# The router's columns as the stationary operand for six of eight token blocks

## The chip, the core and the metric

One NeuronCore of a Trainium2 chip runs the whole program. TensorE (PE; its weight loads are listed apart as PEld) multiplies, VectorE (DVE), ScalarE (ACT) and GpSimd (POOL) work on tiles in SBUF and PSUM, and SyncE (SP) issues most DMAs. The metric is the device time of one execution in microseconds (us), lower is better.

## The reference, cut to what matters

One encoder layer over 1024 tokens of width 1024, all in float32: differential attention, then a hierarchical mixture of 16 experts in four groups, then a final norm. The change touches the router, which turns each token's normed and modulated row into 4 group logits and 16 expert logits:

```python
def hier_moe(h, w_rg, b_rg, w_re, b_re, w_gate, w_up, w_down):
    t = h.reshape(B * S, D)
    g_logits = (t @ w_rg).astype(jnp.float32) + b_rg
    g_idx = jnp.argmax(g_logits, axis=-1)
    e_logits = jnp.einsum('td,dge->tge', t, w_re).astype(jnp.float32) + b_re
    e_sel = jnp.take_along_axis(e_logits, g_idx[:, None, None], axis=1)[:, 0]
    top_v, top_i = lax.top_k(e_sel, EXPERT_TOP_K)
```

The logits of a token pick one group and two of its experts, so nothing of the experts can begin before the last token's logits have been ranked and the tokens have been gathered.

## The kernel before, in words

Tokens are worked in 8 blocks of 128 (`t` = 0 to 7, `TB` = 8). Attention runs first (up to about 650 us). The stage in question, the generator `post_gen` (from L657), follows and runs to about 740 us; its first pieces are interleaved with the last of attention. For each block t it does:

- `chunk(t, 0)` and `chunk(t, 1)`: the output projection of one half of 512 columns. Each is 24 matmuls on 128x512 (L693) into one of two PSUM buffers `mm`; then DVE does L702, L703, L704 (gate, residual, scale) and ACT squares the rows for the norm (L705, L707 or L709 and L710). The row's reciprocal root `r` comes out of the second half alone.
- `trans(t - 1, 0)` and `trans(t - 1, 1)`, between the two halves of block t: PE turns over the eight 128x128 pieces of the block before (L722), the first four into the PSUM buffer `tp`, the other four into the PSUM buffer `av`; ACT copies each four to `h2T` in SBUF (L723, `Q<-tp` and `Q<-av`). `tp` and `av` are one buffer each.
- `router(t - 1)`, after the second half: eight matmuls in full float32, each two passes in the records (16 records, L735). `h2T[:, k]`, 128 tokens, is the stationary operand and the 20 router columns `wr20[:, k]` move; the result, 128 tokens x 20, goes to `tp`. DVE scales it by `r`, adds the bias and writes `L[:, t]` (L737).
- `write_h2(t - 1)`: DVE finishes the normed rows (L729) and SP stores them (L730).

Block 7 is cut finer: after `chunk(7, 0)` and the turn-over of block 6 the second half goes in two quarters (`last_sums`, L806, 24 matmuls of 256 columns each), and `routing()` is stepped in between. Its `ranks(0, 6)` (L922 to L928) ranks the logits of blocks 0 to 5 on DVE; matmuls L954 to L959 on PE count them and need L928's result; then come the turn-over of half of block 7 (L826), the router of block 6 (L735 into `av`), and the second quarter. Blocks 6 and 7 are ranked at the end, then the tokens of expert 0 are gathered.

What sets the order: PE runs in the order in which the code is written, with no exception (`manual_schedule` on PE for the whole program). DVE, ACT, POOL and SP are ordered by a list scheduler with a cost model, except in the last stretch (from L795), where ACT and DVE too keep the order of the code. Every engine takes its instructions in order, so that an instruction that waits holds up those behind it.

Of the kernel before, what the change touches and what calls it, by code (L numbers as in the profile page):

```python
# [4 lines left out]
F32 = mybir.dt.float32  # L5
# [5 lines left out]
OP = mybir.AluOpType  # L11
# [4 lines left out]
P = 128  # L16
S = 1024
D = 1024
KT = D // P
TB = S // P  # L20
# [15 lines left out]
def build(tc, x, c, ada_w, ada_b, norm_mix, norm_ffn, w_in, lq1, lk1, lq2, lk2, subln, w_out,  # L36
          rgw, rgb, rew, reb, wg, wu, wd, norm_final, out, dbg=None):
    nc = tc.nc
# [21 lines left out]
    ident = const.tile([P, P], F32, name="ident")  # L60
# [19 lines left out]
    st = tc.alloc_tile_pool(name="start", bufs=1)  # L80
# [4 lines left out]
    def ps_mm():  # L85
        return ps.tile([P, 512], F32, name="mm", bufs=2)

    def ps_tp():
        return ps.tile([P, 4, P], F32, name="tp")

    def ps_av():
        return ps.tile([P, 512], F32, name="av")
# [108 lines left out]
    for t in range(TB):  # L201
# [8 lines left out]
        for kk in range(2):  # L210
# [4 lines left out]
            for i in range(4):  # L215
                k = kk * 4 + i
# [124 lines left out]
    at = tc.alloc_tile_pool(name="attn", bufs=1, reuse_waits="tile")  # L341
# [97 lines left out]
    now = [0]  # L439
# [217 lines left out]
    def post_gen():  # L657
        st = {}
# [20 lines left out]
            nc.scalar.copy(oH, orw)  # L679
            (nc.vector if t in OLD else nc.gpsimd).tensor_tensor(oL, orw, f(oH), op=OP.subtract)  # L680

        L = RT0["L"] = at.tile([P, TB, 20], F32, name="L", tag="vt")
        cst = at.tile([P, 3, D], F32, name="K", bufs=2)
        load(0, 0)
        load(1, 0)
# [10 lines left out]
        def chunk(t, n, py=None):  # L696
            ns = slice(n * 512, (n + 1) * 512)
            if py is None:
                py = ps_mm()
                yield from sums(t, n, py, range(H))  # L700
            a, xt, sq, rst = st[t][2:6]
            nc.vector.tensor_tensor(a[:, ns], py, g1b[:, ns], op=OP.mult)  # L702
            nc.vector.tensor_tensor(xt[:, ns], xt[:, ns], a[:, ns], op=OP.add)  # L703
            nc.vector.tensor_tensor(a[:, ns], xt[:, ns], s2b[:, ns], op=OP.mult)  # L704
            nc.scalar.activation(py, xt[:, ns], AF.Square, accum_out=sq[:, n:n + 1])  # L705
            if n == 0:
                nc.scalar.activation(sq[:, 0:1], sq[:, 0:1], AF.Identity, scale=1.0 / D, bias=epst)  # L707
            else:
                nc.scalar.activation(rst, sq[:, 1:2], AF.Ln, scale=1.0 / D, bias=sq[:, 0:1])  # L709
                nc.scalar.activation(rst, rst, AF.Exp, scale=-0.5)  # L710
                nc.sync.dma_start(accd[t * P:(t + 1) * P], xt)
# [15 lines left out]
        def write_h2(t):  # L727
            a, rst = st[t][2], st[t][5]
            nc.vector.scalar_tensor_tensor(a, a, rst, sh2b, op0=OP.mult, op1=OP.add)  # L729
            nc.sync.dma_start(h2d[t * P:(t + 1) * P], a)  # L730

        def router(t, ks, pl):
            h2T = st[t][6]
            for k in ks:
                nc.tensor.matmul(pl, h2T[:, k], wr20[:, k], start=(k == 0), stop=(k == KT - 1))  # L735
            if k == KT - 1:
                nc.vector.scalar_tensor_tensor(L[:, t], pl, st[t][5], br20, op0=OP.mult, op1=OP.add)  # L737
            for k in ks:
                yield

        def pl_tp():
            return ps_tp().rearrange("p a b -> p (a b)")[:, 0:20]

        def load_next(t):

# [18 lines left out]
        def block(t):  # L764
            if t == 0:
                yield from first()
                return
            yield from chunk(t, 0)
            yield from trans(t - 1, 0)
            yield from trans(t - 1, 1)  # L770
            if t < TB - 1:
                yield from chunk(t, 1)
                yield from router(t - 1, range(KT), pl_tp())
                write_h2(t - 1)

        for t in range(TB):
# [9 lines left out]
            for _ in block(t):  # L786
                if t:
                    load_next(t + 1)
                yield
        t = TB - 1  # L790
        a, xt, sq, rst = st[t][2:6]
        rt = routing()
        next(rt)
# [27 lines left out]
        h2T = at.tile([P, KT, P], F32, name="Q", bufs=3)  # L821
# [15 lines left out]
        pl = ps_mm()[:, 0:20]  # L837
# [14 lines left out]
    RT0 = {}  # L852
# [154 lines left out]
    wr20 = misc.tile([P, KT, 20], F32, name="wr20")  # L1007
    nc.sync.dma_start(wr20[:, :, 0:4], rgw[0].rearrange("(k p) g -> p k g", p=P))
    nc.sync.dma_start(wr20[:, :, 4:20], rew[0].rearrange("(k p) g e -> p k (g e)", p=P))
    br20 = misc.tile([P, 20], F32, name="br20")  # L1010
# [12 lines left out]
    n = 5  # L1023
# [7 lines left out]
    for i, (h, qb) in enumerate(seq):  # L1031
# [6 lines left out]
        n = RATE.get(i, n)  # L1038
# [685 lines left out]
```

## Time and profile before

| what | value |
|---|---|
| device time, median of 3 runs | 1216.61 us (1216.36 to 1218.6) |
| the profiled execution | 1216.69 us, of which the recorded span is 1214.9 us |
| PE busy | 1107.9 us, 91% of the span |
| PE weight loads busy | 917.9 us, 76% |
| DVE busy | 942.5 us, 78% |
| ACT busy | 727.2 us, 60% |
| POOL busy | 262.4 us, 22% |
| mean granted clock of PE | 0.962 |

The times in the rows are us from the span's start. The share of a whole span hides that stages have different limits: the stage of the change is the stretch from 650 to 741 us and is read by itself. Matmul records are pipelined, so that a record is longer than its share of the engine; the spacing between the starts of weight loads (PEld) says what one costs. [...]

### The profile page before, as it was taken

What the parts mean: (1) busy time and instruction counts of PE and PEld (TensorE: products, weight loads), DVE (VectorE), ACT (ScalarE), POOL (GpSimd) and SP (SyncE); (2) the same over time, 40 slices, a digit from 0 to 9 for tenths busy, and PEclk for the clock granted to TensorE, in tenths of its full rate; (3) what the DMA queues carried; (4) which work ended last, traced back from release to release, by engine and by line L of the source; (5) the groups of instructions that cost most, each with busy time, mean ns of one, the idle gap of its engine ahead of it and who ended that gap; (6) DMA issues with size and microseconds to landing.
All of it is one profiled execution on the core that took longest, in us unless ns stands there. A gap on an engine that the chain in (4) does not pass through costs nothing. (4 is left out here: it accounts for less than half of the span.)

```text
span 1214.9 us, 19164 instructions
## 1 busy us (share of the span) xinstructions
PE 1107.9 (91%) x6760; PEld 917.9 (76%) x6760; DVE 942.5 (78%) x1560; ACT 727.2 (60%) x1206; POOL 262.4 (22%) x283
## 2 busy tenths in 40 slices
PE   4889999999999999999889995999999999999990
PEld 3667877777787787777678885887888887888880
DVE  5969789888888777687884657798877898777774
ACT  5566666757666676767664323566565667455563
POOL 3011011111101111113402402433222232222121
PEclk8899999999999999999899996899999999999995
DMA  9712022322323110112407734699979899877745
GB/s 328 216 53 82 23 87 87 90 86 83 99 92 89 46 40 27 29 42 91 143 27 226 264 121 147 220 333 336 294 225 303 252 345 336 280 228 227 217 132 223
DMA packets 153255, 199.55 MB, mean 164 GB/s; under 512 B 12967, under 2 KB 124232, under 8 KB 153138
## 3 DMA queue, kind: packets, MB, share of 16 engines
q1 hardware_dynamic: 146432, 179.86, 45.3%
q0 software_dynamic: 6512, 17.68, 6.1%
q8 instruction: 63, 1.03, 0.3%
q10 hardware_dynamic: 194, 0.54, 0.1%
q14 instruction: 54, 0.44, 0.1%
HBM read 175.77 MB, written 27.67 MB: 167 GB/s over the span
## 5 line engine op out<-in xcount | busy, mean ns | idle before, releaser
L1122 DVE TENSOR_TENSOR wlo<-wraw,whi 128x1024 fp32r<-128x1024 f32 x187 | 224.7, 1231 | 23.9 <-ACT whi L1117 13.9
L1385 PE MATMUL gu<-whi,XT 128*128 128x256 f32 x1216 | 209.6, 285 | 2.7
L1117 ACT CAST whi<-wraw 128x1024 fp32r<-128x1024 f32 x192 | 193.2, 1049 | 7.7 <-ACTq L1540 5.0
L486 ACT ACTIVATE E<-E,mn 128x1024 f32<-128x1024 f32 x128 | 147.1, 1151 | 83.3 <-DVE mn L483 83.1
L1385 PEld LDWEIGHTS gu<-whi,XT 128*128 128x128 f32 x1216 | 172.5, 191 | 9.9 <-issue 6.2
L483 DVE CUSTOM_DVE_ANT_0 E<-S,negd 128x1024 f32<-128x1024 f32 x128 | 152.8, 1219 | 18.9 <-PE S L478 18.2
L1385 PE MATMUL gu<-wlo,XT 128*128 128x256 f32 x704 | 148.4, 289 | 1.9 <-POOL wlo L1122 1.9
L285 PE MATMUL mm<-hH,wh 128*128 128x512 f32 x336 | 139.3, 415 | 2.1 <-DVE V L384 2.1
L285 PE MATMUL mm<-hL,wh 128*128 128x512 f32 x336 | 140.3, 417 | 0.0
L285 PE MATMUL mm<-hH,wl 128*128 128x512 f32 x336 | 138.8, 413 | 0.0
L143 POOL TENSOR_TENSOR wl<-wraw,wh 128x1024 fp32r<-128x1024 f32 x21 | 50.4, 2401 | 325.8 <-ACT wh L142 285.5
L513 ACT CAST aH<-tp 128x512 fp32r<-128x512 f32 x128 | 74.0, 578 | 73.9 <-PE tp L511 73.7
L1385 PEld LDWEIGHTS gu<-wlo,XT 128*128 128x128 f32 x704 | 109.8, 191 | 2.4 <-POOL wlo L1122 2.1
L497 DVE SCALAR_TENSOR_TENSOR E<-E,r 128x1024 f32<-128x1024 f32 x64 | 85.8, 1340 | 27.8 <-ACT E L495 26.3
L514 DVE TENSOR_TENSOR aL<-tp,aH 128x512 fp32r<-128x512 f32 x128 | 87.9, 687 | 17.3 <-ACT aH L513 16.1
L1417 PE MATMUL py<-whi,hid 128*128 128x512 f32 x256 | 92.1, 422 | 4.1 <-ACT hid L1407 1.4
L511 PE MATMUL tp<-ident,E 128*128 128x128 f32 x512 | 78.9, 277 | 10.4 <-DVE aL L514 7.2
L511 PEld LDWEIGHTS tp<-ident,E 128*128 128x128 f32 x512 | 62.5, 142 | 33.5 <-DVE aL L514 13.6
L693 PE MATMUL mm<-wo,wh 128*128 128x512 f32 x240 | 80.1, 408 | 1.3 <-ACT mm L705 1.3
L285 PEld LDWEIGHTS mm<-hH,wh 128*128 128x128 f32 x336 | 63.5, 189 | 18.3 <-issue 5.1
L285 PEld LDWEIGHTS mm<-hH,wl 128*128 128x128 f32 x336 | 63.5, 189 | 17.1 <-issue 7.9
L285 PEld LDWEIGHTS mm<-hL,wh 128*128 128x128 f32 x336 | 63.4, 189 | 16.9 <-issue 8.0
(342 smaller groups left out, 2230.2 us busy)
## 6 DMA issues: line engine op xcount, KB each, us to landing
wraw<-in_expert_w_gate SPq DMA_DIRECT2D x64, 512.0 KB
wraw<-in_expert_w_up SPq DMA_DIRECT2D x64, 512.0 KB
wraw<-in_expert_w_down SPq DMA_DIRECT2D x64, 512.0 KB
aw<-in_ada_w SPq DMA_DIRECT2D x64, 256.0 KB
wraw<-in_attn_w_in SPq DMA_DIRECT2D x23, 512.0 KB
ld<-in_ada_w SPq DMA_DIRECT2D x32, 256.0 KB
ld<-in_x SPq DMA_DIRECT2D x8, 512.0 KB
xt<-in_x SPq DMA_DIRECT2D x8, 512.0 KB
```

Of the source, the lines that this page charges most:

```text
L285: nc.tensor.matmul(pq, w[:, k], t[k][:, n], start=(k == 0 and i == 0), stop=(k == KT - 1 and i == 2))
L483: nc.vector.tensor_tensor_reduce(out=e, in0=sps[m], in1=negd[:, w0:w0 + S], op0=OP.add, op1=OP.min, scale=-slope, scalar=3.0e38, accum_out=mn)
L486: nc.scalar.activation(e, e, AF.Exp, bias=mn, scale=-1.0, accum_out=sm)
L497: nc.vector.scalar_tensor_tensor(es[0], es[1], r2, es[0], op0=OP.mult, op1=OP.add)
L511: nc.tensor.transpose(pt[:, i], a[:, k * P:(k + 1) * P], ident)
L513: nc.scalar.copy(th[:, kk * 4:kk * 4 + 4, q], pt)
L514: nc.vector.tensor_tensor(tl[:, kk * 4:kk * 4 + 4, q], pt, f(th[:, kk * 4:kk * 4 + 4, q]), op=OP.subtract)
L693: nc.tensor.matmul(py, w[:, h], wt[h][:, ns], start=(h == 0 and s == 0), stop=(h == H - 1 and s == 2))
L1117: nc.scalar.copy(WP[e, i][0], RAW[e, i])
L1122: eng.tensor_tensor(low, RAW[e, i], f(high), op=OP.subtract)
L1385: nc.tensor.matmul(pg[:, i], XT[:, xi, k], w[:, k % 4], start=(k == 0 and xi == 0 and wi == 0 and i == 0), stop=(k == KT - 1 and (xi, wi) ...
L1417: nc.tensor.matmul(py[n], hT[:, xi, i], WP[e, 8 + hf * 2 + i][wi][:, n * 512:(n + 1) * 512], start=(hf == 0 and j == 0), stop=(hf == 1 and ...
```

## The change

For blocks 0 to 5 the roles in the router's matmul are exchanged. `router_t` holds the 20 columns of `wr20[:, k]` in the array and moves the 128 tokens of `h2T[:, k]` past them, so that the result is 20 x 128 in `tp`; ACT copies it to a strip of SBUF (`lts`, two places in turn). One block later `logits` turns the strip over on PE (a transposition of 20 x 128 to 128 x 20), and DVE reads that as L737 did before. The transposition stands between `trans(t - 1, 1)` and `chunk(t, 1)` and goes to `av`; that of block 5 stands after the turn-over of block 6, ahead of `routing()`. Blocks 6 and 7 keep the old form. The strip and `L` share one tile.

```diff
-        L = RT0["L"] = at.tile([P, TB, 20], F32, name="L", tag="vt")
+        lts = at.tile([P, 512], F32, name="L", tag="vt")
+        L = RT0["L"] = lts[:, 0:TB * 20].rearrange("p (t n) -> p t n", t=TB)
...
+        def router_t(t):
+
+            h2T = st[t][6]
+            pl = ps_tp().rearrange("p a b -> p (a b)")
+            for k in range(KT):
+                nc.tensor.matmul(pl[0:20, 0:P], wr20[:, k], h2T[:, k], start=(k == 0), stop=(k == KT - 1))
+                yield
+            lt = lts[0:20, 256 + t % 2 * P:256 + t % 2 * P + P]
+            nc.scalar.copy(lt, pl[0:20, 0:P])
+            LT[t] = lt
+
+        def logits(t):
+            pl = ps_av()[:, 0:20] if now[0] >= 65 else ps_tp().rearrange("p a b -> p (a b)")[:, 0:20]
+            nc.tensor.transpose(pl, LT[t], ident[0:20, 0:20])
+            nc.vector.scalar_tensor_tensor(L[:, t], pl, st[t][5], br20, op0=OP.mult, op1=OP.add)
+
+        LT = {}
+
...
-        def pl_tp():
-            return ps_tp().rearrange("p a b -> p (a b)")[:, 0:20]
...
             if t < TB - 1:
+                if t - 2 in LT:
+                    logits(t - 2)
                 yield from chunk(t, 1)
-                yield from router(t - 1, range(KT), pl_tp())
+                yield from router_t(t - 1)
                 write_h2(t - 1)
...
         t = TB - 1
+        logits(t - 2)
         a, xt, sq, rst = st[t][2:6]
         rt = routing()
         next(rt)
```

In the changed program the lines behind the edit have other numbers: L722 is L723, L693 is L694, the transposition is L746, the DVE step behind it L747, the ACT copy of the strip L741, and `ranks` is L941 to L947.

PE, between the two halves of block 2, before (the waits are those on other engines' semaphores; `av<-ident,hrow` is the second half of the turn-over):

```order
L693 MATMUL mm<-wo,wl 128x512
L722 MATMUL tp<-ident,hrow 128x128 [waits DVE_49]
L722 MATMUL tp<-ident,hrow 128x128 x3
L722 MATMUL av<-ident,hrow 128x128 [waits DVE_49]
L722 MATMUL av<-ident,hrow 128x128 x3
L693 MATMUL mm<-wo,wh 128x512 [waits Activation_49]
L693 MATMUL mm<-wo,wh 128x512
```

The same place on PE in the changed program:

```order
L694 MATMUL mm<-wo,wl 128x512
L723 MATMUL tp<-ident,hrow 128x128 [waits Activation_49]
L723 MATMUL tp<-ident,hrow 128x128 x3
L723 MATMUL av<-ident,hrow 128x128 [waits DVE_49]
L723 MATMUL av<-ident,hrow 128x128 x3
L746 MATMUL av<-ident,L 128x20 [waits Activation_49]
L694 MATMUL mm<-wo,wh 128x512 x2
```

One instruction has come in, it writes the buffer that the four ahead of it wrote, and it waits for ACT. It stands at this place six times (in blocks 2 to 6 and ahead of L806 in block 7).

DVE, in blocks 6 and 7, before: from the logits of block 5 (L737) to the first steps on `chunk(7, 0)`, with `ranks(0, 6)` (L922 to L928) between them:

```order
L737 SCALAR_TENSOR_TENSOR L<-tp,r_6786,br_738 128x20
L703 TENSOR_TENSOR xt<-xt,hrow 128x512
L922 TENSOR_TENSOR K<-L 128x480
L704 TENSOR_TENSOR hrow<-xt,K 128x512
L923 TENSOR_TENSOR K<-L 128x480
L924 TENSOR_TENSOR K<-K 128x480
L925 TENSOR_TENSOR K<-K 128x480
L926 TENSOR_REDUCE K<-K 128x120
L927 TENSOR_TENSOR K<-K 128x120
L928 TENSOR_TENSOR rk<-K 128x96
L702 TENSOR_TENSOR hrow<-mm,K 128x512
L703 TENSOR_TENSOR xt<-xt,hrow 128x512
```

DVE in the changed program, from the last step on `chunk(7, 0)` (L705) over the logits of block 5 (L747) to the end of `ranks(0, 6)`; L826 to L828 are the steps of the first quarter:

```order
L705 TENSOR_TENSOR hrow<-xt,K 128x512
L747 SCALAR_TENSOR_TENSOR L<-av,r_6795,br_738 128x20
L941 TENSOR_TENSOR K<-L 128x480
L942 TENSOR_TENSOR K<-L 128x480
L943 TENSOR_TENSOR K<-K 128x480
L826 TENSOR_TENSOR hrow<-mm,K 128x256
L944 TENSOR_TENSOR K<-K 128x480
L827 TENSOR_TENSOR xt<-xt,hrow 128x256
L945 TENSOR_REDUCE K<-K 128x120
L828 TENSOR_TENSOR hrow<-xt,K 128x256
L946 TENSOR_TENSOR K<-K 128x120
L947 TENSOR_TENSOR rk<-K 128x96
```

The ranks of six blocks stood ahead of DVE's steps on `chunk(7, 0)`; now they stand behind them, mixed with those of the first quarter. On PE the matmuls that need them (L954 before, L973 now) still stand right behind the first quarter.

## Rows read from the trace of the kernel before

**Rows 1.** By stretch: us, busy PE, PEld, DVE, ACT, POOL (instructions), clock, DMA, GB/s.

```profile
650.00:700.00 50.00, 50.00 (x277) 43.12 (x277) 27.54 (x29) 19.13 (x41) 17.49 (x7) 1.00 0.84 273
700.00:739.00 39.00, 39.00 (x249) 34.46 (x247) 22.31 (x40) 10.88 (x28) 2.39 (x1) 1.00 0.27 99
...
741.00:775.00 34.00, 19.85 (x136) 18.20 (x136) 28.56 (x72) 13.41 (x22) 18.86 (x27) 0.60 0.56 180
775.00:1198.00 423.00, 388.22 (x2807) 344.16 (x2805) 337.90 (x489) 251.47 (x378) 115.25 (x156) 0.98 0.87 274
```

**Rows 2.** Timeline of PEld, 651 to 656: start, us, engine, line, tiles, shape, count.

```profile
651.60 0.19 PEld L526 LDWEIGHTS av<-aL,V 128*128 128x128 f32 x1
651.72 0.19 PEld L527 LDWEIGHTS av<-aH,V 128*128 128x128 f32 x1
...
652.67 1.99 PEld L735 LDWEIGHTS tp<-wr,Q 128*128 128x128 f32 x16
...
654.57 0.30 PEld L693 LDWEIGHTS mm<-wo,wh 128*128 128x128 f32 x2
...
655.16 0.42 PEld L537 LDWEIGHTS av<-sq,ones 128*128 128x128 f32 x2
...
655.61 0.41 PEld L693 LDWEIGHTS mm<-wo,wh 128*128 128x128 f32 x2
```

**Rows 3.** Timeline, the turn between the halves of block 2, PEld and ACT.

```profile
660.94 0.47 PEld L722 LDWEIGHTS av<-ident,hrow 128*128 128x128 f32 x4
...
661.25 0.59 ACT L723 COPY Q<-tp 128x512 f32<-128x512 f32 x1 [3.41 <-PE tp L722]
661.38 0.30 PEld L693 LDWEIGHTS mm<-wo,wh 128*128 128x128 f32 x2
...
661.73 0.59 ACT L723 COPY Q<-av 128x512 f32<-128x512 f32 x1
```

**Rows 4.** Timeline, a turn-over on PE that waited for such a copy.

```profile
641.60 0.57 ACT L723 COPY Q<-tp 128x512 f32<-128x512 f32 x1
642.23 0.42 PEld L511 LDWEIGHTS tp<-ident,E 128*128 128x128 f32 x4 [1.35 <-ACT Q L723]
```

**Rows 5.** Timeline of block 7, DVE and PE: last step of its first half to `last_sums(1)`'s end.

```profile
731.52 0.68 DVE L704 TENSOR_TENSOR hrow<-xt,K 128x512 f32<-128x512 f32 x1
...
732.54 0.22 PE L954 MATMUL S<-rk,K 128*128 128x96 bf16 x1
...
732.73 0.42 DVE L807 TENSOR_TENSOR hrow<-mm,K 128x256 f32<-128x256 f32 x1 [0.53 <-PE mm L806]
...
738.01 1.38 PEld L940 LDWEIGHTS <-rk 128*128 128x128 bf16 x12
```

**Rows 6.** Timeline of DVE, the logits of block 5 and `ranks(0, 6)`.

```profile
723.39 0.24 DVE L737 SCALAR_TENSOR_TENSOR L<-tp,r,br 128x20 f32<-128x20 f32 x1 [1.00 <-PE tp L735]
...
724.15 0.65 DVE L922 TENSOR_TENSOR K<-L 128x480 f32<-128x480 f32 x1
...
727.26 0.65 DVE L926 TENSOR_REDUCE K<-K 128x120 f32<-128x480 f32 x1
...
728.02 0.28 DVE L927 TENSOR_TENSOR K<-K 128x120 f32<-128x120 f32 x1
...
728.34 0.26 DVE L928 TENSOR_TENSOR rk<-K 128x96 bf16<-128x96 f32 x1
```

**Rows 7.** PE by stretch about one fall of its granted clock: busy, clock, DMA share.

```profile
585.20:587.40 2.20, 0.52 (x5) 1.00 0.55 115
587.40:590.90 3.50, 2.26 (x10) 0.51 0.00 0
```

**Rows 8.** Timeline of PEld, four router loads at the lower clock.

```profile
741.54 0.93 PEld L735 LDWEIGHTS mm<-wr,Q 128*128 128x128 f32 x4 [0.30 <-ACT Q L827]
```

**Rows 9.** What PE waited for from 741 to 800: us in total, times, longest.

```profile
PE xt L1278 <- DMA xgxa<-h2d,rk: 5.1, 1, 5.1
...
PE gu L1385 <- POOL wlo L1122: 1.9, 1, 1.9
```

## What the change was expected to do

> **What bounds the kernel now.** I read the busy time by stretch first. From 650 to 739 us, where all the turns of the router lie, PE is busy for the whole of both stretches at the full granted clock, while DVE and ACT are busy for about half of the time or less [rows 1]. PE sets the pace there: what is added to PE's queue, or makes PE stand still, lengthens the stage, and what is taken from DVE or ACT is worth nothing. From 741 to 775 us PE is busy for 19.85 of 34 us, and its longest wait, 5.1 us, is for the gathered tokens of expert 0 [rows 9]; these come out of the ranking at the end of the stage, so a later end of the stage is a later gather. From 775 to 1198 us PE is busy for 388 of 423 us [rows 1]: a delay has no hole there to vanish in. So each us that PE loses between 650 and 741 us should come out at the end. The second view is the timeline of one turn between the halves of a block [rows 3], the third that of block 7 with the ranking [rows 5, 6].
>
> **The router's matmuls.** Before, 16 passes per block: their weight loads begin at 652.67, the next line's at 654.57, 1.90 us [rows 2], 0.119 a pass, although only 20 columns move; the stationary 128x128 that is loaded for each pass is what takes the time. In the new form 128 columns move. The trace has full-float32 passes of the same kind in L537: two passes of 256 moved columns from 655.16 to 655.61, 0.225 a pass [rows 2], so 0.11 for 128 columns if it goes by columns. 16 of them are 1.8 us: what is saved on loading is spent on moving. I take 0.1 us saved a block, 0.6 us in all. The bounds: nothing saved, or, if such a pass ran at the pace of L526, which moves 256 columns of the one-pass type in 0.12 us (651.60 to 651.72) [rows 2], 0.06 for 128 and 0.96 for 16, 0.94 saved a block, 5.6 us in all. L537 is the row of the same type, so I stay at its end.
>
> [...]
>
> **The new wait in each turn.** `logits` puts one transposition on PE right behind the four of `trans(t - 1, 1)`. It writes `av`, which those four have just filled, so it must wait until ACT has copied `av` out. ACT's copy of `tp` runs from 661.25 and that of `av` from 661.73 to 662.32, while PE went on with `chunk(t, 1)` at 661.38 [rows 3]. A turn-over that waits for such a copy starts 0.06 us after the copy's end (642.17 to 642.23) [rows 4], here at 662.38; its load occupies 0.11 (four loads in 0.44, 660.94 to 661.38) [rows 3]; `chunk(t, 1)` then begins at 662.49 instead of 661.38, 1.1 us later. Queued behind it are the 24 matmuls of `chunk(t, 1)`, and behind those DVE's L702, the next router and the next block. ACT can't be earlier: it is idle for 3.4 us before the copies [rows 3] and waits for PE itself. The turns of the other blocks have the same spacing, so five of them, in blocks 2 to 6, cost 5 x 1.1 = 5.5 us. The bounds are 1.0 (no load of its own) and 1.2.
>
> **The last turn.** `logits` of block 5 stands in block 7. DVE reads its result behind L704, which ends at 731.52 + 0.68 = 732.20 [rows 5] (times as in the trace of before, without the delay so far), and `ranks(0, 6)` can begin only then; before, it began at 724.15, behind the first L737, and ended at 728.60 [rows 6], 4 us ahead of L954, which therefore did not wait. That cover is gone. Now: 732.20 + 0.24 for the logits [rows 6], five operations of 128x480, L922 to L926, at 0.65 or 0.66 (first and last shown), 3.26 [rows 6], L927 and L928 0.28 + 0.26 [rows 6], and in between, by the changed order, three steps of the first quarter at 0.42, 1.26 [rows 5]: 737.50. PE is let go 0.06 later, at 737.56, where L954 began at 732.54 [rows 5]: 5.0 us, of which 1.1 is the turn and 3.9 a second wait. Queued behind L954 on PE are the turn-over of half of block 7, the router of block 6 and the whole second quarter, until 738.01 [rows 5]; all of the ranking's end hangs on them. Bounds: 4.5 if DVE's records overlap, 5.5 if each hand-over costs a little.
>
> **The clock.** A wait of 3.9 us is long enough to cost more than itself. At 585.2 to 587.4 PE worked for 0.52 of 2.20 us and the granted clock then fell to 0.50, 1.2 GHz, for the next 3.5 us [rows 7]. At that level four router loads take 0.93 us [rows 8], against 1.90 for sixteen, twice as much. Behind the wait lie 738.01 - 732.54 = 5.5 us of PE work [rows 5]. Bounds: 0 if the clock stays up, 5.5 if all of it runs at half. If half the level lasts for 3.5 us of it, the loss is 1.75; it began with PE at work there, and the work behind our wait begins with light matmuls, so I expect two such stretches: 3.5 us.
>
> **Edits at nothing.** ACT's copy of 20x128 (six, less than the 0.59 of a 128x512 copy [rows 3]) stands on ACT behind L705 and ahead of L709; the next thing PE needs from ACT is the copy in the next turn, some 5 us on, and ACT is busy for 19 of 50 us [rows 1]. On DVE the wait for the router of 1.00 us ahead of each L737 [rows 6] goes; DVE is not what PE waits for, so it yields nothing. The list scheduler also puts one output-projection load and a residual store in another place on SP and one splitting step a place later on POOL; PE waited for none of these from 650 to 739 us [rows 1], and I put them at 0, at worst 1 us.
>
> **Sum.** Against the profiled execution, 1216.69 us (span 1214.9; the median is 1216.61, so no correction): -0.6 + 5.5 + 5.0 + 3.5 = +13.4, 1230.1 us.
>
> **Rivals.**
> - *The clock stays up* in the last wait: +9.9, 1226.6. For: PE is busy up to the wait. Against: [rows 7], where a shorter pause was followed by the fall.
> - *The clock falls in the turns too.* Each turn would put about 0.9 us of standing still next to 0.9 us of turn-overs. For each fall 3.5 us at half cost 1.75; in three of six turns that is 5.3, 1235.4. Against: the turns of before, with the same turn-overs and the router's light matmuls, pass without a fall from 650 to 739 us [rows 1], and 0.9 us is about half of the pause in [rows 7]. [...]
> - *Moving 128 columns is cheap*: the pace of L526, 5.6 saved instead of 0.6, 1225.1. Against: L537.
> - *Not slower: the delay is absorbed behind the stage.* Between 741 and 775 us PE stands for 14 us. If these were waits for the experts' weights, which stream whatever the tokens do, a delay up to 14 us would vanish and only the router's 0.6 us would be left, 1216.1. It decides from the point where the weights come later than the tokens. Against: 5.1 us are for the gather, and only 1.9 for a weight tile (L1122) [rows 9].
> - *It doesn't do what it says*: PE would not wait in the turn, because the copy is early. The order shows the wait, the timeline its end.
>
> **How the numbers follow.** Chances: forecast 0.60, clock stays up 0.15, clock falls in the turns 0.12, cheap moving 0.06, absorbed 0.04, some way to a gain 0.03. With the bounds of the forecast's own terms (clock 0 to 5.5, last turn 4.5 to 5.5) it reaches from 1226 to 1233; the two neighbours put the range at 1225 to 1236. A measurement of this kernel tells about 0.2%, 2.4 us, from no change: slower by more than that 0.93, within 0.04, faster 0.03.
>
> **What would show it.** In the changed profile: PE idle 0.9 to 1.0 us, ended by ACT's `Q`, six times in front of L746; the spacing of the new router's loads near 0.11; PE idle about 3.9 us in front of L973, ended by DVE; a granted clock of 0.50 in the microseconds behind it; and from the gather on the same picture as before, later by the sum. I am wrong if L746 starts with no wait, if the new passes come at 0.06 us, or if the gather is late and the end is not.

## The result, and the profile after

The changed kernel takes 1232.13 us (median of four runs, 1230.71 to 1233.42) against 1216.91 us for the kernel before beside it: a ratio of 1.0120, 95% interval 1.0105 to 1.0134. The profiled execution took 1232.95 us, 16.3 us more than that of before. 1230.1 us had been forecast. In all that follows a line number is that of the kernel named; in the changed kernel the turn-over is L723, its copies L724, a chunk's matmuls L694, the new router L738, the transposition of the logits L746.

By stretch (us, busy PE, PEld, DVE, ACT, POOL with instructions, granted clock, DMA share, GB/s), changed kernel:

```profile
650.00:700.00 50.00, 47.81 (x258) 38.69 (x257) 23.33 (x27) 18.39 (x40) 15.44 (x6) 1.00 0.82 266
700.00:739.00 39.00, 36.82 (x192) 29.44 (x190) 18.35 (x21) 10.66 (x31) 5.45 (x2) 1.00 0.25 95
743.80:754.04 10.24, 9.30 (x54) 9.30 (x54) 2.42 (x12) 1.29 (x4) 0.00 (x0) 0.50 0.01 2
791.00:1214.00 423.00, 388.47 (x2809) 344.29 (x2807) 337.60 (x489) 251.72 (x378) 115.98 (x156) 0.98 0.87 274
```

PE, which was busy for every microsecond from 650 to 739 [rows 1], now stands still for 4.4 us of it, and then works through a stretch of 10.24 us at the lower clock. From the expert phase on nothing has changed: 388.47 us of PE work in 423, as against 388.22 [rows 1], only 16 us later. The waits of PE from 640 to 800 us (who, for whom, us in total, times, longest):

```profile
PE av L746 <- ACT Q L724: 4.4, 6, 0.7
PE xt L1297 <- DMA xgxa<-h2d,rk: 3.9, 1, 3.9
PE idx L1262 <- DVE aux L1238: 3.0, 1, 3.0
PE S L973 <- DVE rk L947: 3.0, 1, 3.0
```

The first and the last line are new. Behind the stage the wait for the gathered tokens (second line) became 1.2 us shorter, 3.9 instead of 5.1 us [rows 9], and the next one, for DVE's cast L1238 (L1219 before), 1.2 us longer, 3.0 instead of 1.8 us, so that the two cancel; the one for POOL's split tile (L1404) is 1.9 us as before [rows 9]. One turn, PEld and ACT (answers to [rows 3]):

```profile
661.15 0.59 PEld L723 LDWEIGHTS tp<-ident,hrow 128*128 128x128 f32 x4
661.70 0.47 PEld L723 LDWEIGHTS av<-ident,hrow 128*128 128x128 f32 x4
...
662.49 0.59 ACT L724 COPY Q<-av 128x512 f32<-128x512 f32 x1
...
663.13 0.13 PEld L746 LDWEIGHTS av<-ident,L 20*128 20x128 f32 x1 [0.96 <-ACT Q L724]
663.30 0.30 PEld L694 LDWEIGHTS mm<-wo,wh 128*128 128x128 f32 x2
```

From the turn-over into `av` to the next chunk's load 0.44 us passed before (660.94 to 661.38 [rows 3]); now it is 1.60 (661.70 to 663.30). The transposition starts 0.05 us behind the end of ACT's copy (663.08). All six turns have this spacing.

The router of block 0, PEld (answers to [rows 2]):

```profile
653.05 0.19 PEld L694 LDWEIGHTS mm<-wo,wl 128*128 128x128 f32 x1
653.48 1.65 PEld L738 LDWEIGHTS tp<-Q,wr 128*20 128x20 f32 x16 [0.24 <-PE av L527]
655.34 0.30 PEld L694 LDWEIGHTS mm<-wo,wh 128*128 128x128 f32 x2 [0.21 <-issue]
```

The shape tells it: the stationary is now 128x20. The sixteen passes are quick, but PEld stands still for 0.24 us ahead of them (0.35 us in the other five blocks) and for 0.21 us behind them; before, it was 0.04 us at most.

The last turn and what is behind it: DVE, then PEld (answers to [rows 5, 6, 8]):

```profile
739.40 0.69 DVE L705 TENSOR_TENSOR hrow<-xt,K 128x512 f32<-128x512 f32 x1
...
740.27 0.66 DVE L941 TENSOR_TENSOR K<-L 128x480 f32<-128x480 f32 x1
...
744.43 0.26 DVE L947 TENSOR_TENSOR rk<-K 128x96 bf16<-128x96 f32 x1
```

```profile
741.57 0.10 PEld L973 LDWEIGHTS <-K 128*128 128x128 bf16 x1
744.74 0.34 PEld L975 LDWEIGHTS <-K 128*128 128x128 bf16 x5 [3.08 <-issue]
...
745.86 3.54 PEld L754 LDWEIGHTS av<-wr,Q 128*128 128x128 f32 x16
...
754.36 1.38 PEld L959 LDWEIGHTS <-rk 128*128 128x128 bf16 x12
```

PE is ready at 741.57 and let go at 744.74, when the ranks of blocks 0 to 5 are done. The sixteen passes of the old router behind it then take 3.54 us instead of 1.86 us before (733.25). The way from there to the index matmuls (L959, L940 before) is 9.62 us (744.74 to 754.36), against 5.47 (732.54 to 738.01 [rows 5]).

**Where the 16.3 us went.** The first full turn starts 0.76 us later than before (661.15; 660.39 there), of which 0.26 is the router of block 0 (from the load ahead of it to the load behind it); 0.5 us lies ahead of the change. Four kernels below that are the same as the one before up to that turn (e9_widths, e11_one_split, e12_two_splits, e13_modes) begin it between 659.53 and 661.51, so 0.5 us is within what one execution differs from another. Six routers at 0.26: 1.6. Six turns at 1.16: 7.0. The wait for the ranks: 3.0. The work behind it: 9.62 - 5.47 = 4.15. Together 16.25.

### The profile page after: what moved, and what is told of

The parts are those of the page before. It is cut to its first block, busy times and chain, and to the rows that moved or that the text cites. A ratio compares the mean times of both kernels' runs of the same rounds, so it can differ in the third digit from the quotient of the medians.

```text
span 1231.2 us, 19183 instructions
## 1 busy us (share of the span) xinstructions
PE 1115.5 (91%) x6766; PEld 920.3 (75%) x6766; DVE 944.3 (77%) x1560; ACT 728.6 (59%) x1212; POOL 263.4 (21%) x283
## 5 line engine op out<-in xcount | busy, mean ns | idle before, releaser
L1404 PE MATMUL gu<-whi,XT 128*128 128x256 f32 x1216 | 209.4, 285 | 2.7
L1404 PEld LDWEIGHTS gu<-whi,XT 128*128 128x128 f32 x1216 | 172.4, 191 | 10.0 <-issue 5.3
L1404 PE MATMUL gu<-wlo,XT 128*128 128x256 f32 x704 | 148.4, 289 | 1.9 <-POOL wlo L1141 1.9
L1404 PEld LDWEIGHTS gu<-wlo,XT 128*128 128x128 f32 x704 | 109.7, 191 | 2.4 <-POOL wlo L1141 2.1
L694 PE MATMUL mm<-wo,wh 128*128 128x512 f32 x240 | 80.5, 410 | 1.3 <-ACT mm L706 1.3
```

The source lines that it names most:

```text
L694: nc.tensor.matmul(py, w[:, h], wt[h][:, ns], start=(h == 0 and s == 0), stop=(h == H - 1 and s == 2))
L1404: nc.tensor.matmul(pg[:, i], XT[:, xi, k], w[:, k % 4], start=(k == 0 and xi == 0 and wi == 0 and i == 0), stop=(k == KT - 1 and (xi, wi) ...
```

## Experiments

The times of one kernel spread over 1.7 to 6.1 us here, so the timed ratios tell apart only the larger effects. The blocks are far more regular: from the first turn-over of one block to that of the next it is 13.627 us before, to 0.001, in four of five cases (13.667 once), and 15.060 after, in all five. Where a few tenths of a us matter I read this period.

### The stationary as wide as the array (e1_wide)

```diff
-    ones = misc.tile([P, P], F32, name="ones")
+    wrp = misc.tile([P, KT * 20 + P], F32, name="wr20")
+    ones = wrp[:, KT * 20:]
...
-                nc.tensor.matmul(pl[0:20, 0:P], wr20[:, k], h2T[:, k], start=(k == 0), stop=(k == KT - 1))
+                nc.tensor.matmul(pl[:, 0:P], wrp[:, k * 20:k * 20 + P], h2T[:, k], start=(k == 0), stop=(k == KT - 1))
...
```

> The changed kernel, but with a stationary of 128 columns instead of 20 in the router's new form: the tile behind the 20 columns is read along, and the 108 further rows of the result are ignored (the tile behind the last of them is the constant of ones). Nothing else changes. Theory 1 (the change of the stationary's width is what costs: the load of the first narrow pass is not issued behind a running matmul of full width, nor the first full load behind the last narrow pass): the distance from the router's first weight load to the next chunk's first falls from 2.39 us (mean of six) to about 2.05, some 0.3 us less a block, 1.8 us less in all, to about 1230.3 us. Theory 2 (the moved columns themselves, or the yield to another line, cost it): 2.39 stays within 0.05, and the time stays at 1232 us. The spacing of the passes, 0.109 us, should not change in either.

PEld at the router of block 0, e1_wide:

```profile
653.27 0.19 PEld L695 LDWEIGHTS mm<-wo,wl 128*128 128x128 f32 x1
653.39 1.98 PEld L739 LDWEIGHTS tp<-Q,wr 128*128 128x128 f32 x16
655.29 0.30 PEld L695 LDWEIGHTS mm<-wo,wh 128*128 128x128 f32 x2
```

Both pauses are gone. From the load ahead to the load behind it is 2.02 us, as in the kernel before; the changed kernel has 2.29. The period falls to 14.740, 0.32 us less, with five equal ones. Of the 0.32 us, 0.27 lie at the router and 0.05 in the chunk behind it (5.34 us; 5.39 in the changed kernel). Theory 1 holds, but for a detail: the spacing of the passes did not stay at 0.109. With the full stationary it is 0.112 us behind a first step of 0.23 us (1.90 for sixteen, 653.39 to 655.29, or 0.119 on average), and that is so whether 128 columns move, as here, or 20, as in the kernel before. Timed: 1231.27 us, ratio to before 1.0109 (1.0089 to 1.0129), too close to the changed kernel to tell 1.8 us.

### What each shape costs (e9_widths, e13_modes)

```diff
+        def probe(t):
+            p = ps_av()
+            h = st[t - 1][6][:, 0]
+            if t == 2:
+                nc.tensor.matmul(p[0:20, 0:P], wr20[:, 0], h, start=True, stop=True)
+            elif t == 3:
+                nc.tensor.matmul(p[:, 0:P], ident, h, start=True, stop=True)
+            elif t == 4:
+                nc.tensor.transpose(p[:, 0:20], ident[0:20], ident[0:20, 0:20])
+            elif t == 5:
+                nc.tensor.transpose(p[:, 0:P], h, ident)
...
+                py = ps_mm()
+                yield from sums(t, 1, py, range(4))
+                if t > 1:
+                    probe(t)
+                yield from sums(t, 1, py, range(4, H))
...
```

> The kernel before with one piece of work that nobody reads put in the middle of the second chunk of each of five blocks, a different one in each; what each adds to the block's period of 13.627 us is its price. Block 2: one matmul in full float32 (two passes) with a stationary of 128 rows x 20 columns and 128 moved columns. Block 3: the same with a stationary of 128x128. Block 4: a transposition with 20 rows x 128 columns in the array. Block 5: a transposition of 128x128. Block 6: four matmuls as in block 2, eight passes in a row. Theory 1 (a price for each change of the stationary's shape, none for the passes behind it): block 2 adds 0.22 us for two passes and about 0.32, 0.54; block 3 adds 0.24; block 4 adds 0.375; block 5 adds 0.11; block 6 adds 0.87 and the same 0.32 once, 1.2. Theory 2 (each narrow pass is dearer): block 6 adds four times what block 2 adds. Theory 3 (shape has no price, the router and the transposition lose to something else around them): blocks 2 and 3 add the same, and so do 4 and 5.

e13_modes has one matmul in each block instead, of `r` rows and `c` columns:

```diff
+            c, r = {2: (64, P), 3: (72, P), 4: (96, P), 5: (P, 64), 6: (P, 96)}[t]
+            nc.tensor.matmul(p[0:c, 0:P], ident[0:r, 0:c], h[0:r], start=True, stop=True)
```

> As e9_widths (the kernel before, with one matmul that nobody reads in the middle of the second chunk of five blocks, full float32, two passes of 128 moved columns), now with other shapes of the stationary: 128 rows x 64 columns in block 2, 128 x 72 in block 3, 128 x 96 in block 4, 64 rows x 128 columns in block 5, 96 x 128 in block 6. A full 128x128 added 0.253 us to the period there, one of 128x20 0.566. [...] Theory 2 (any stationary that is not 128x128 costs it): all five add 0.5 or more. Theory 3 (only very narrow ones do): none of the five adds more than 0.3.

These two kernels ran once each (1220.98 and 1217.43 us), and only the period is read from them; each price comes from one block of one execution. What each added to the period of 13.627 us:

| in the array (rows x columns) | added, us |
|---|---|
| 128x128, two passes | 0.253 |
| 128x96, two passes | 0.253 |
| 128x72, two passes | 0.253 |
| 96x128, two passes | 0.253 |
| 128x64, two passes | 0.593 |
| 64x128, two passes | 0.640 |
| 128x20, two passes | 0.566 |
| 128x20, eight passes | 1.246 |
| 128x128, one transposition | 0.160 |
| 20x128, one transposition | 0.386 |

PEld in e13_modes, the load of the probe (L745) in blocks 2 to 6; what stands in brackets is the pause ahead of it:

```profile
663.88 0.19 PEld L745 LDWEIGHTS av<-Q,ident 128*64 128x64 f32 x2 [0.35 <-issue]
...
677.78 0.37 PEld L745 LDWEIGHTS av<-Q,ident 128*72 128x72 f32 x2
...
691.66 0.40 PEld L745 LDWEIGHTS av<-Q,ident 128*96 128x96 f32 x2
...
705.86 0.29 PEld L745 LDWEIGHTS av<-Q,ident 64*128 64x128 f32 x2 [0.35 <-issue]
...
719.81 0.42 PEld L745 LDWEIGHTS av<-Q,ident 96*128 96x128 f32 x2
```

72 and 96 columns, and 96 rows, cost what 128 do, to the thousandth. 64 of either cost 0.34 to 0.39 us more, and 20 columns 0.31. The price is paid once, for the way in and out together: six passes more in a row add 1.246 - 0.566 = 0.68, 0.113 each. So theory 1 of e9_widths is borne out. In e13_modes theory 2 fails with 72 and 96, which added 0.253 us and not 0.5 or more, and theory 3 with the 64s, which added 0.593 and 0.640 us. What stands between them is a step, between 64 and 72 columns and, for rows, between 64 and 96; the rows show it and the pause of 0.35 us ahead of either stationary of 64, and not what makes it.

### The turn: another buffer, another place (e2_tp, e4_turns)

```diff
-            pl = ps_av()[:, 0:20] if now[0] >= 65 else ps_tp().rearrange("p a b -> p (a b)")[:, 0:20]
+            pl = ps_tp().rearrange("p a b -> p (a b)")[:, 0:20]
```

> The changed kernel, but every turned strip of logits goes into tp, the buffer of the first four turn-overs, instead of av, the buffer of the last four; it then waits for the earlier of ACT's two copies. Theory 1 (the wait in the turn is for ACT's copy of the buffer that is written, and its length is the distance to that copy's end): from the first turn-over of the second four to the next chunk's first load 1.60 us now, becomes about 1.1, 0.48 us less in each of six turns, 2.9 us in all; to about 1229 us if the end of the ranking keeps its place. Theory 2 (the transposition costs by itself, whatever it waits for): 1.60 stays. The order on DVE also changes, since its step on the logits comes a place earlier, so that the wait in front of the count of the ranks may change too; it is read apart.

PEld and ACT in the turn of block 2, e2_tp:

```profile
662.44 0.59 ACT L724 COPY Q<-av 128x512 f32<-128x512 f32 x1
662.59 0.13 PEld L746 LDWEIGHTS tp<-ident,L 20*128 20x128 f32 x1 [0.47 <-ACT Q L724]
662.76 0.30 PEld L694 LDWEIGHTS mm<-wo,wh 128*128 128x128 f32 x2
```

The transposition now starts behind the first copy, which began at 661.96 and took 0.59, and before the second has ended; the turn is 1.11 us (661.65 to 662.76) and the period 14.613, 0.447 less. Theory 1 holds: the length of the turn is set by the copy whose buffer is written. The wait in front of the ranks became 3.3 us: DVE's long step (L730, 1.28 us) now stands among the ranks instead of ahead of them. Timed: 1230.70 us, 1.0108 (1.0091 to 1.0125).

```diff
             if t < TB - 1:
+                py = ps_mm()
+                yield from sums(t, 1, py, range(4))
                 if t - 2 in LT:
                     logits(t - 2)
-                yield from chunk(t, 1)
+                yield from sums(t, 1, py, range(4, H))
+                yield from chunk(t, 1, py)
```

> The changed kernel, but the transposition of the logits of blocks 0 to 4 stands in the middle of the next half's 24 matmuls instead of in front of them, when ACT's copies have long been done. The last one, in front of the second half of block 7, stays as it is. Theory 1 (each turn costs 1.16 us because PE stands still for ACT's copy): the turns of blocks 2 to 6 go back from 1.60 to about 0.44 us, the transposition itself costs 0.1 to 0.3 in its new place, and the time falls by 4.3 to 5.3 us, to about 1227.3. Theory 2 (what the turns lose is made up for, or lost again, behind them: PE then waits for the router's copy or a PSUM buffer): less than 2 us of it comes out at the end. The wait of 3.0 us for the ranks and the fall of the clock in block 7 are left as they are by theory 1.

PEld in block 3, e4_turns:

```profile
677.95 0.47 PEld L723 LDWEIGHTS av<-ident,hrow 128*128 128x128 f32 x4
...
678.39 0.30 PEld L694 LDWEIGHTS mm<-wo,wh 128*128 128x128 f32 x2
...
681.32 0.13 PEld L746 LDWEIGHTS av<-ident,L 20*128 20x128 f32 x1 [0.35 <-issue]
681.49 0.30 PEld L694 LDWEIGHTS mm<-wo,wh 128*128 128x128 f32 x2
```

The turn is back at 0.44 us and ACT's copy holds nobody up. The period is 14.280: 0.78 less than with the turn, not 1.16, since the transposition costs 0.38 even where nothing waits, the 0.386 of the table above. Five of these are 3.9 us in the stage (the last turn starts 75.30 us behind the first in the changed kernel, 71.40 here). At the end only 1.9 of them show (span 1229.3; 1231.2): this execution was 1.97 us later before the first full turn. And PE's wait for a split weight tile of expert 0 was 3.9 us instead of 1.9, a thing to which I come back below. Timed: 1230.39 us, 1.0112 (1.0091 to 1.0134). Theory 1 is borne out in the stage; that its gain arrives at the end whole isn't shown by this run. The later start and the longer wait alone would have left nothing of it; what helped is that the granted clock fell three times for 3.4 us in the expert phase (780 to 1203 us), and four times in the changed kernel.

### The clock (e3_fill)

```diff
+        dp = ps_tp().rearrange("p a b -> p (a b)")
+        for i in range(NFILL):
+            nc.tensor.matmul(dp, st[t][0][:, i % 4], WO[0][i % 4][:, 0:512], start=True, stop=True)
```

> The changed kernel with twelve matmuls of 128x512 more on PE, in the place where it waits 3.0 us for the ranks of blocks 0 to 5; nobody reads what they give. Theory 1 (the granted clock falls because PE stands still there, and the fall costs the 4.15 us that the work behind takes longer): the granted clock stays at 1.00 from 740 us to the end of the second quarter, the way from the count of the ranks to the index matmuls goes from 9.6 us back to about 5.5, the count itself begins when it did (2.7 us of work in a wait of 3.0), and the time falls by about 4 us, to 1228. Theory 2 (the work behind the wait is late for reasons of its own, by waits on DVE and ACT, and the clock is only seen beside it): the way stays near 9 us and the time at 1232.

By stretch, and PEld of the same place, e3_fill:

```profile
743.80:754.04 10.24, 9.71 (x90) 8.97 (x88) 4.28 (x16) 2.96 (x11) 0.00 (x0) 1.00 0.13 53
```

```profile
741.69 2.60 PEld L852 LDWEIGHTS tp<-wo,wh 128*128 128x128 f32 x12
744.55 0.10 PEld L977 LDWEIGHTS <-K 128*128 128x128 bf16 x1 [0.26 <-issue]
...
745.67 1.87 PEld L755 LDWEIGHTS av<-wr,Q 128*128 128x128 f32 x16
...
750.43 1.38 PEld L963 LDWEIGHTS <-rk 128*128 128x128 bf16 x12
```

The count of the ranks begins as it did in the changed kernel (744.55; 744.74 there), but with work instead of a pause ahead of it the granted clock stays at 1.00, the old router takes 1.87 us instead of 3.54, and the index matmuls follow 5.88 us behind the count of the ranks instead of 9.62. Theory 1 holds, with 3.74 us. Twelve matmuls that nobody reads made the kernel faster. Timed it is 1225.17 us (1222.06 to 1228.07), 1.0066 (1.0046 to 1.0086): about 7 us less than the changed kernel, more than the 3.74. In the profiled execution the rest lies in the expert phase: from its first turn-over to the end 456.2 us (764.56 to 1220.76) against 462.5 in the changed kernel (768.61 to 1231.16). The same columns for that phase, e3_fill and then the changed kernel:

```profile
788.70:1205.00 416.30, 380.15 (x2783) 337.22 (x2781) 337.96 (x489) 251.62 (x379) 117.05 (x156) 0.99 0.88 279
```

```profile
781.40:1215.00 433.60, 396.14 (x2861) 351.75 (x2859) 347.01 (x503) 255.70 (x383) 121.39 (x160) 0.97 0.86 272
```

The granted clock was 0.99 there, not 0.97. The changed kernel's execution stood at 0.50 four times for 3.4 us in this phase (from 788.2, 883.7, 1061.2 and 1129.5 us), that of e3_fill not once from 778.2 to 1194.5; at half the pace (3.54 us for the old router against 1.87, above) four such stretches cost an estimated 6.8 us, half of 4 x 3.4. The kernel before has four of them too. Why the clock held here is open; the variation among this kernel's own runs is as large as the gain.

### The last turn alone (e5_last)

```diff
-            yield from chunk(t, 0)
+            if t == TB - 1:
+                py = ps_mm()
+                yield from sums(t, 0, py, range(4))
+                logits(t - 2)
+                yield from sums(t, 0, py, range(4, H))
+                yield from chunk(t, 0, py)
+            else:
+                yield from chunk(t, 0)
...
-        logits(t - 2)
```

> The changed kernel, but the transposition of block 5's logits alone stands in the middle of the first half of block 7, ahead of the turn-over of block 6, so that the ranks of blocks 0 to 5 can begin as early as in the kernel before. Blocks 2 to 6 keep their turns of 1.60 us. Theory 1 (the three losses of block 7 hang on one place): its turn gives back 1.16 us less the 0.375 us that such a transposition costs in the middle of a chunk (worked out from the blocks' period of 14.280 us when it stands there, against 15.060 with the turn), the wait of 3.0 us for the ranks goes, and with it the fall of the clock and its 4.15 us: 7.9 us less than the changed kernel, about 1224.2 us. Theory 2 (the clock falls at the end of the stage whatever stands there): only 3.8 us less, 1228.3. Theory 3 (the ranks, early again, hold up DVE's steps on block 7, for which PE then waits): less than 3 us less.

By stretch, and PEld of block 7, e5_last:

```profile
735.00:748.00 13.00, 13.00 (x115) 12.34 (x113) 9.86 (x25) 3.44 (x10) 0.00 (x0) 1.00 0.10 42
```

```profile
740.59 0.10 PEld L979 LDWEIGHTS <-K 128*128 128x128 bf16 x1
...
741.30 1.87 PEld L754 LDWEIGHTS av<-wr,Q 128*128 128x128 f32 x16
...
746.07 1.03 PEld L965 LDWEIGHTS <-rk 128*128 128x128 bf16 x9
```

PE is busy for all of 13 us, at the full clock; the count of the ranks does not wait, and the index matmuls stand at 746.07, 8.0 us earlier than in the changed kernel once the 0.30 us by which this execution was ahead is taken off. Timed: 1223.96 us, 1.0059 (1.0039 to 1.0079); 1224.2 had been worked out. Theory 1 holds: one transposition, in one place, made half of the loss.

### Everything taken away (e7_full), and what was left (e10_split, e11_one_split, e12_two_splits)

e7_full joins the edits of e1_wide, e4_turns and e5_last, and transposes in full:

```diff
-            lt = lts[0:20, 256 + t % 2 * P:256 + t % 2 * P + P]
-            nc.scalar.copy(lt, pl[0:20, 0:P])
+            lt = lts[:, 256 + t % 2 * P:256 + t % 2 * P + P]
+            nc.scalar.copy(lt, pl[:, 0:P])
...
-            nc.tensor.transpose(pl, LT[t], ident[0:20, 0:20])
+            nc.tensor.transpose(pl, LT[t], ident)
```

> The changed kernel with all its losses taken away as they are understood so far: a stationary of 128 columns in the router's new form (the 108 further columns of the result are nobody's), all six transpositions in the middle of a chunk, and each of them a full 128x128 one (ACT copies 128x128 for it, of which 20 rows are the logits). Theory 1 (a change of the stationary's shape is what costs, in the router 0.32 us a block and in a transposition of 20 rows most of its 0.375): the period of a block is 13.627 us, as before the change, plus 0.11 for one full transposition, 13.74; the time is that of the kernel before plus 6 x 0.11 = 0.7, about 1217.5 us. Theory 2 (the transposition costs its 0.375 us whatever its shape): a period of 14.00 and 2.3 us more than the kernel before, 1219.1. If the form itself gained anything, the period would be under 13.627.

By stretch, and the one new thing among PE's waits, e7_full:

```profile
650.00:739.00 89.00, 89.00 (x526) 77.57 (x524) 51.30 (x68) 30.64 (x75) 20.90 (x8) 1.00 0.59 197
```

```profile
PE gu L1414 <- POOL wlo L1151: 4.9, 1, 4.9
```

The period is 13.700, PE stands still nowhere in the stage, and the index matmuls (738.43) come 0.42 us behind those of before [rows 5]. The losses in the stage are gone: with wide shapes the exchanged form costs 0.07 us a block more than the old one. The chunk with the transposition takes 0.127 us longer (5.470; 5.343 before), the router 0.007 less and the chunk behind it 0.047 less; why that chunk is shorter is open. On the whole the form gains nothing. Yet the time is 1220.67 us, 1.0031 (1.0019 to 1.0044), where 1217.5 had been worked out: 3 us are missing between the medians (the profiled execution, 1218.57 us, was 1.9 us above that of before). What is new behind the stage is the longer wait for a split weight tile of expert 0 (1.9 before [rows 9]). POOL, in the kernel before, at two of the twelve small steps ahead of that tile:

```profile
761.82 0.33 POOL L1251 TENSOR_SCALAR tt<-ax,rk 128x2 f32<-128x2 f32 x1
...
764.65 0.20 POOL L1255 TENSOR_TENSOR tt<-ax 128x2 f32<-128x2 f32 x1
```

The same two in e7_full:

```profile
762.48 1.39 POOL L1280 TENSOR_SCALAR tt<-ax,rk 128x2 f32<-128x2 f32 x1
...
766.57 1.07 POOL L1284 TENSOR_TENSOR tt<-ax 128x2 f32<-128x2 f32 x1
```

Steps of two elements a partition take 0.18 to 0.53 us or over 1 us. In both traces every long one ends 0.04 to 0.06 us behind the end of one of DVE's splits of 128x1024 (761.82 us, for example, is in a pause of DVE's splitting; the step at 762.48 ends at 763.87, DVE's split at 763.82), and no short one lasts through such an end; the same program order, begun 0.4 us later, meets them otherwise. Of the twelve, six are long in e7_full and four before; the seven and five in the text for e10_split below are miscounted. To test it, POOL's splitting was moved to DVE, in e7_full (e10_split) and in the kernel before (e12_two_splits; e11_one_split moves the first step alone):

```diff
-    split_lo(0, 3, nc.gpsimd)
+    split_lo(0, 3)
...
-        split_lo(0, 4, nc.gpsimd)
+        split_lo(0, 4)
```

> The kernel e7_full, with two splitting steps of expert 0 (the low halves of its weight tiles 3 and 4, 128x1024 each) on DVE instead of POOL. In e7_full PE waits 4.9 us for such a tile from POOL, where it waited 1.9 us before the change; POOL's twelve small steps ahead of it took 0.18 to 0.53 us or 1.07 to 1.39 us each, seven of them long there, five before. Theory 1 (what e7_full loses beyond the 0.44 us that its stage is later is only this wait: POOL's small steps stretch whenever they fall beside DVE's splitting): with POOL's splitting gone the wait goes, and this kernel stands to the kernel before with the same two steps moved (e12_two_splits, run beside it) within 1 us. Theory 2 (the 3 us come from the new form of the router in another way): it stays 3 us above that kernel.

> The kernel before the change, with both splitting steps of expert 0 that POOL does there (weight tiles 3 and 4) on DVE. Theory 1: as e11_one_split, and PE's wait of 1.9 us for tile 4 from POOL goes too, since DVE does such a step in 1.21 us when POOL is quiet: 2 to 4 us less than the kernel before, about 1214. Theory 2 (DVE becomes the bound: it splits seven tiles from 759.7 to 771.6 us already, and two more of 1.2 us each make the last ones late): no gain, or up to 2.4 us more.

> The kernel before the change, with one splitting step of expert 0 (weight tile 3) on DVE instead of POOL. In the trace of before, a cast of 128x128 on DVE took 3.70 us beside that step of POOL, 0.38 us the two times when POOL was not splitting, and PE then waited 2.25 us for it. Theory 1 (the cast waits for POOL's step): the cast takes 0.38 us, the wait of PE goes, the splitting step costs DVE 1.2 us, and the time falls by 1 to 2.2 us, to about 1215. Theory 2 (PE is bound a few us later by the split tiles anyway, 1.9 us of waiting for tile 4): the gain goes into that wait, and the time stays.

| kernel | median, us | ratio to the kernel before (95%) |
|---|---|---|
| e10_split | 1217.98 | 1.0013 (1.0003 to 1.0023) |
| e12_two_splits | 1217.51 | 1.0008 (0.9995 to 1.0022) |
| e11_one_split | 1213.95 | 0.9975 (0.9963 to 0.9988) |

e10_split lies 0.5 us above e12_two_splits: what is left of the exchanged form is about the 0.4 us of the stage, and the 3 us went with POOL's splitting (theory 1). In both kernels PE then waits for the gather of expert 1's tokens (5.1 and 4.3 us), so they are compared under that new wait and not under none. For e12_two_splits theory 1 failed: the wait for the tile is gone, but PE waits 4.3 us for the gather of expert 1's tokens instead, so nothing is gained. The time is theory 2's, the place is not: it is the gather, and not DVE's last tiles, that is late. POOL's small steps ahead of this gather are long again, five of the last six (1.06 to 1.28 us), beside DVE's splitting.

e11_one_split is 2.8 us faster than the kernel before, and so the fastest of all here. The size is theory 1's, the way only in part. DVE's cast, before and in e11_one_split:

```profile
752.77 3.70 DVE L1219 CAST aux<-rk 128x128 bf16<-128x128 f32 x1
```

```profile
753.17 1.63 DVE L1219 CAST aux<-rk 128x128 bf16<-128x128 f32 x1
```

It fell to 1.63 us, not to 0.38, and what PE gained on it (1.8 to 1.0 us of waiting) it lost on the next step of DVE (0.4 to 1.5 us). What went is the wait of 1.9 us for the split tile, which no longer appears among PE's waits, and with it a fall of the granted clock: from 771.80 to 775.15 us it is 0.50 in the kernel before, right behind that wait, and 1.00 in e11_one_split.

## Why the prediction was right, point by point

- **What bounds the stage, and that the delay passes whole.** Right. PE's lost time from 650 to 754 us comes out where the gather is issued (747.7 and 764.1, 16.4 us later) and at the end (16.3). The rival in which it is absorbed has no hole in any trace. But it is not the gather alone that holds expert 0 back: PE had its tokens only 15.2 us later (753.52; 768.72), and the 1.2 us won there were lost in the next wait, for DVE's cast, so that the index matmuls behind it (L1243; L1262) began 16.4 us later.
- **The wait in each turn.** Right in mechanism, place and size: 1.1 us forecast, 1.16 measured, six times. e2_tp shows that it is the copy of the buffer that is written. What I did not see is that the transposition of 20 rows costs 0.386 us where nothing waits, 0.23 more than a full one, so that this part stays when the wait goes; in the turn most of it is hidden in the wait (0.17 us from its load to the next, 663.13 to 663.30, where 0.11 had been counted).
- **The last turn.** Right in mechanism; the term was mis-sized. The wait was put at 3.9 us and is 3.0. The step at fault is the sum of durations on DVE: from the start of L705 to the end of the last rank it was put at 5.98 us and took 5.29 (739.40 to 744.69). Records of DVE overlap: the step of 0.66 us at 740.27 is followed at 740.85, 0.58 later, and one of 0.42 us at 741.99 by the next at 742.32. The bound for that, 4.5 for the last turn, was set (4.2 measured, with the turn's 1.16), and was too narrow.
- **The clock.** Right in mechanism; the term was mis-sized, and that 3.5 came so near the 4.15 measured is luck. The lower level held for 10.24 us, through nearly the whole of the 5.5 us of work, and not for two stretches of 3.5. The trace of before could have told: behind the stretch of [rows 7] the clock stayed down for two more rows, 10.3 us in all.

```profile
590.90:594.30 3.40, 2.00 (x7) 0.50 0.43 104
594.30:597.70 3.40, 3.40 (x11) 0.50 0.99 323
```

In the second of these rows matmuls of 512 columns came 0.427 us apart (596.00 and 596.43 us), 1.2 columns a ns, which is what the trace shows of the 1.2 GHz in the prediction; behind it they came 0.231 us apart (597.70 and 597.93 us). In the changed kernel the lower level did not cost the 5.5 us of the bound; the second quarter's passes, for one, slow down by less than two: three of them take 0.64 us at the lower level (749.28 to 749.92) and 0.36 at the full one (748.16 to 748.52 in e3_fill). e3_fill shows that the pause is the cause. The turns, with 0.96 us of pause each, brought no fall, as expected (1.00 from 650 to 739 us); the rival of falls there is out.
- **The router's matmuls.** Wrong, in sign: 0.6 us saved was forecast, 1.6 us more measured. The step that failed is not the one that had been doubted. The passes do come at 0.109 us, so L537 was the right row and "moving is cheap" is out. But I compared passes with passes and took the way in and out of them at nothing; a stationary of 20 columns costs 0.31 us there. The bounds, nothing to 5.6 us saved, did not hold it, and a bound below nothing should have been kept, for the trace of before had rows that speak for one. In attention, PEld stands still ahead of a stationary of 64 rows in 64 places, 23.3 us in all, 0.36 each (line, busy us and mean ns, idle us ahead):

```profile
L478 PEld LDWEIGHTS S<-K,Q 64*128 64x128 f32 x256 | 19.0, 184 | 23.3 <-issue 23.3
```

And at the end of the stage itself L940 loads 128x128 and 128x64 in turn, twelve loads in bf16 0.117 us apart (738.01 to 739.41), where L959 loads 128x128 alone every 0.025 us (from 732.71 on). That loading the stationary is what takes a pass's time, as the prediction has it, no run shows: with loads of 20 columns the passes came at 0.109 us, with loads of 128 at 0.112.
- **Edits at nothing.** ACT's copy of the strip and the logits on DVE held nobody up. Half a us lay ahead of the change, within what one execution differs from another.

The errors partly cancel, by luck: +2.2 for the router, -0.9 for the wait, +0.65 for the clock, +0.4 for the turns, +0.5 from ahead of the stage. The sum of 13.4 us became 16.3 in the profiled execution and 15.2 between the medians.

## What to carry to other kernels

Before a small matrix is made the stationary operand, look at its shape and not only at its size: between float32 passes, in these runs, 72 or more columns and 96 rows went in like the full array, while 64 of either and 20 columns cost 0.31 to 0.39 us on the way in and out, more than the sixteen passes gave back (the router as a whole took 0.26 us longer). An instruction put on a busy engine has to stand where its input is long done, since one that waits holds up what is queued behind it (the next chunk's first load came 1.16 us later in each turn); the middle of the next run of matmuls did it here at no wait. And a pause on TensorE is priced by what is behind it: 3.0 us of waiting cost 4.15 us more at the lower clock, and filling the pause with useless matmuls gave 3.7 us of it back.

## What the runs showed of the hardware that was not expected

- The step in the price of a stationary between 64 and 72 columns (for rows, between 64 and 96), above; from 72 to 128 columns the price is the same to 0.001 us.
- POOL's smallest steps took 0.18 to 0.53 us or 1.05 to 1.39 us, in the same program order, by where they fell beside DVE's work, and DVE's cast of 128x128 took 0.38 us or 3.70 us (752.77 to 756.47) beside POOL's splitting (753.88 to 756.24 us). PE's wait for the split tile behind them was 1.6 us (e3_fill) to 4.9 us (e7_full) in the kernels where POOL splits both tiles and this wait was read, and none in e10_split, e11_one_split and e12_two_splits; that is the size of single terms of this study. POOL's long steps end 0.04 to 0.06 us behind the end of one of DVE's splits, above. The cast ran from within POOL's own casts (752.70 us on) to 0.23 us behind the end of its split; what held either isn't shown.
